# Memory queries and keys as seven-product granules, and attention's token granules as pairs of 512-column products

## The chip, the cores and the metric

One core of a Trainium2 chip. The metric is device time of one launch in microseconds (us), the median of several runs. The engines are named as in the profile: PE is TensorE's matmul stream, PEld its weight loads, DVE is VectorE, ACT is ScalarE, POOL is GpSimd, SP is the engine that issues most DMAs.

## The reference, cut to what matters

The program is one layer of a hybrid trunk over 640 tokens (128 context, 512 latent), width 1024, all in float32: a feed-forward half step, a token mixer, a second feed-forward half step. The mixer multiplies the normed input `h` with one wide input projection and splits the product:

```
mq, mk, mv, mo, mg, dq, dk, dv, gm, gd = split_cols(h @ p['w_in'][l])
att = diff_attention(rope_2d(rmsnorm(dq)), concat(rope_2d(rmsnorm(dk)), cache_k), concat(dv, cache_v), lam)
hm  = rmsnorm(mlstm(mq * 256**-0.5, mk, mv, gates(mg)) forward and backward) * sigmoid(mo)
y   = sigmoid(gm) * (hm @ w_br_m) + sigmoid(gd) * (att @ w_br_d)
x   = x + m[5] * (y @ w_out)
```

`mq`, `mk`, `mv`, `mo` have 4 heads of 256 columns (the memory's queries, keys, values and output gates), `dq`, `dk`, `dv` have 8 attention heads of 128 columns, `gm` and `gd` are branch gates of 1024 columns. So every part is made of pieces of 1024 x 256 weights, which the kernel calls granules. The change is only in how and where the granules of `mq`, `mk`, `mv`, `dq`, `dk` and `dv` are multiplied.

## The kernel before

**Products.** Every float32 operand is split into a high part and a low part of a reduced matmul type (`wH`, `wL`; `hH`, `hL`), and one product is three matmuls, high x high, low x high and high x low (`mm3`; all matmuls of it are recorded at line 75). ACT makes the high part (line 51), DVE the low part (line 54, `wL<-raw,wH`).

**Stages.** The program runs the first feed-forward step; the second norm with the first attention projections; the gates stage; attention; the memory stage (the mLSTM); the two branch products and the output product; and the second feed-forward step.

**Gates stage** (`Gates`, a subclass of the seven-product scheme `Winograd`). A granule is cut into halves along each axis and multiplied by a Strassen-like scheme with seven products in place of eight: 84 matmuls of 320 columns (`ps_f<-`), in place of 96. Its work list holds 12 granules: six of `gm`/`gd`, four of `mo`, and head 0 of `mq` and of `mk`. Results go to DRAM (`gm_dram`, `mq_dram` and so on). Beside it, DVE does "columns" tiles, the adaptive-norm products of a later stage, one behind a granule at the places listed in `IN_GATES`; five more such tiles stand in the memory stage.

**Fill units in attention.** Attention's own work leaves PE waiting for softmax, so the remaining granules stand in a queue (`Fill`) and are multiplied in small units between the pieces of attention. A token granule (`tok_units`) yields [tokens x 256 columns] in five units of 24 matmuls of 256 columns (`ps_t`, 128 tokens each). A feature granule (`feat_units`) yields its transpose in four units of 24 matmuls of 320 columns (`ps_p`). Token granules are `k`, `q` of pairs of heads 1 to 3, `v` of pairs 0 to 3 and `mv` of heads 0 to 3; feature granules are heads 1 to 3 of `mq` and `mk`, and the last of `gm` and of `gd`. The split of the granule at the head of the queue must be complete before its first unit; `ahead()` makes the high part of the next one, `aside()` calls `low()` for its low part, and the slots hold two granules (`wp`, `bufs=2`).

**Attention's order.** For each of 8 heads and 5 query blocks the code writes by hand: scores (`H.scores`: PE, 8 matmuls, `sc`), the turn of the previous block's weights (`ps_wT`), softmax (`H.soft`: DVE's `mn<-sc`, line 1619, then ACT's two `p<-sc,mn` exponentials), fill units, the mix (DVE's `p<-p,r,p`), the values' products (`ps_o`), fill units again. `UNITS` says how many units stand at each place: `two` is one ahead of the mix and one behind the values, `one` is one alone, and the last entry of each head is for the end of the head, where the next head's queries and keys are transposed (`ps_qkT`, 10 small matmuls, then DVE's `kH` casts). When a `k` or `q` granule is finished, `qk_norm_rope` norms and rotates it on DVE (`ss`, `ry`, four multiplies and adds of 128x1024 to 128x1280). Ahead of head 0's first scores stands `gate_rows`, the mLSTM's scans on DVE (scans at line 1409, copy of `QA` and others), one part per call of `aside`. `fill.drain(3)` leaves three granules (12 units) to the memory stage.

**Memory stage.** `load` and `load_c` fetch `P`, `va` and `C` by SP's queue; `cell` is a step of one direction of one head; `fill.pace(0.8, 1)` sets how many units stand between cells; `stats` normalises the output of the last head, and then the branch product `w_brd` follows as fill units.

The scheduler of the language reorders what isn't wrapped in `written()`; PE's and SP's instructions keep the program's order.

## Time and profile before

| what | value |
|---|---|
| median of 3 runs (lowest, highest) | 1813.63 us (1813.38, 1814.05) |
| the profiled execution's own time | 1812.29 us |
| its span in the trace | 1810.5 us, so 1.8 us lie outside the span |
| granted TensorE clock | 1.00 |
| busy share of PE, PEld, DVE, ACT | 99%, 96%, 74%, 50% |

Times in the trace count from the start of the span. A row of the chain of waits is a piece of the work that ended last: start, length, engine and line, how many instructions. A row of a timeline is start, length, instruction, and in brackets how long the engine had been idle and what ended that. A row of the windows has for each stretch of time the busy time of PE, PEld, DVE, ACT and POOL with the number of instructions. Matmul records overlap, so the length of one matmul (309 ns for 320 columns) isn't what it costs: the cost is the distance from start to start, which is read from a row that groups many.

### The profile page before, as it was taken

How to read it: one execution, taken by the hardware profiler on the slowest of the kernel's cores; microseconds unless marked ns; L12 is line 12 of the kernel's file. 1: busy time of each engine (PE TensorE's matmuls, PEld its weight loads, DVE VectorE, ACT ScalarE, POOL GpSimd, SP SyncE). 2: the span in 40 equal slices, each digit the busy share in tenths (PEclk: the TensorE clock that was granted, in tenths of full speed). 3: DMA queues.
4: the chain of work that ended last, by engine and by line, in shares of the span. 5: the costliest groups of instructions: out<-in, count | busy, mean ns of one | idle time of the engine just before them, and what ended most of it. 6: DMA issues, size and time to landing. Idle time of an engine off the chain costs nothing.

```text
span 1810.5 us, 30758 instructions
## 1 busy us (share of the span) xinstructions
PE 1784.8 (99%) x12550; PEld 1743.7 (96%) x12550; DVE 1345.2 (74%) x2162; ACT 899.6 (50%) x1579; POOL 41.0 (2%) x72
## 2 busy tenths in 40 slices
PE   8999999999999999999999999999999999999998
PEld 7999999999999999999999998899999999999998
DVE  6889987677888765858585547877668888897485
ACT  5654544333655455656565546562326545554432
POOL 0000000100000000000000000000000000000010
PEclk9999999999999999999999999999999999999999
DMA  8355566977245544221221134565652455557992
GB/s 327 111 198 177 185 232 224 349 227 266 84 139 182 194 143 131 78 70 63 69 69 60 64 106 129 181 248 209 216 173 78 134 174 185 203 179 274 352 310 84
DMA packets 132207, 311.36 MB, mean 172 GB/s; under 512 B 10017, under 2 KB 93217, under 8 KB 119009
## 3 DMA queue, kind: packets, MB, share of 16 engines
q1 hardware_dynamic: 120690, 263.64, 42.2%
q0 software_dynamic: 10688, 43.13, 7.4%
q8 instruction: 98, 1.61, 0.4%
q10 hardware_dynamic: 688, 2.63, 0.4%
q14 instruction: 43, 0.35, 0.1%
HBM read 240.49 MB, written 68.87 MB: 171 GB/s over the span
## 4 chain that ended last, share of the span: by engine, by line
PE 83%; DVE 7%; DMA 5%; ACT 3%; issue 1%; SPq 0%; DVEq 0%; ACTq 0%
PE ps_f L75 49%; PE ps_p L75 13%; PE ps_t L75 12%; PE sc L75 2%; PE ps_o L75 2%; DVE ww L54 2%; DMA raw_a<-in_w_ada_k 1%; PE ps_qkT L78 1%; PE ps_wT L78 1%; DMA P<-nm_dram 1%; PE ps_n L75 1%; DMA raw<-in_w2b 1%; DVE junk L814 1%; PE ps_u L75 1%; DMA a_raw<-aT_dram 1%
## 5 line engine op out<-in xcount | busy, mean ns | idle before, releaser
L75 PE MATMUL ps_f<-S,ww 128*128 128x320 f32 x2400 | 387.1, 310 | 2.7 <-DMA S<-g_dram 0.9
L75 PEld LDWEIGHTS ps_f<-S,ww 128*128 128x128 f32 x2400 | 359.8, 188 | 6.7 <-DVE ww L54 4.6
L54 DVE TENSOR_TENSOR ww<-raw,ww 128x2048 fp32r<-128x2048 f32 (+1 forms) x73 | 163.9, 2245 | 65.9 <-ACT ww L51 65.8
L75 PE MATMUL ps_t<-wH,hH 128*128 128x256 f32 x640 | 185.1, 289 | 0.9 <-DVE x L57 0.9
L75 PE MATMUL ps_f<-hm,ww 128*128 128x320 f32 x1176 | 185.8, 309 | 0.1
L75 PE MATMUL ps_t<-wH,hL 128*128 128x256 f32 x640 | 181.0, 283 | 0.9 <-DVE hL L54 0.9
L75 PE MATMUL ps_t<-wL,hH 128*128 128x256 f32 x640 | 180.9, 283 | 0.0
L75 PEld LDWEIGHTS ps_f<-hm,ww 128*128 128x128 f32 x1176 | 175.7, 188 | 0.6 <-DVE ww L54 0.6
L51 ACT ACTIVATE ww<-raw 128x2048 fp32r<-128x2048 f32 (+1 forms) x73 | 136.8, 1874 | 58.8 <-DVE raw L54 34.9
L54 DVE TENSOR_TENSOR raw<-raw 128x1024 f32<-128x1024 f32 x186 | 160.8, 864 | 2.4
L75 PE MATMUL ps_f<-hm,wB 128*128 128x320 f32 x1008 | 161.5, 309 | 0.0
L75 PE MATMUL ps_p<-hH,wH 128*128 128x320 f32 x480 | 151.1, 315 | 0.7 <-ACT aT L51 0.7
L75 PEld LDWEIGHTS ps_f<-hm,wB 128*128 128x128 f32 x1008 | 151.3, 188 | 0.0
L75 PE MATMUL ps_p<-hH,wL 128*128 128x320 f32 x480 | 148.3, 309 | 0.0
L75 PE MATMUL ps_p<-hL,wH 128*128 128x320 f32 x480 | 148.3, 309 | 0.0
L51 ACT ACTIVATE u<-ps_f 128x320 f32<-128x320 f32 x129 | 55.8, 433 | 156.1 <-PE ps_f L75 155.9
L75 PEld LDWEIGHTS ps_t<-wH,hH 128*128 128x128 f32 x640 | 122.3, 191 | 1.5 <-ACT nsq L51 1.1
L75 PEld LDWEIGHTS ps_t<-wH,hL 128*128 128x128 f32 x640 | 122.4, 191 | 1.1 <-DVE hL L54 1.1
L75 PEld LDWEIGHTS ps_t<-wL,hH 128*128 128x128 f32 x640 | 122.5, 191 | 0.3
L1619 DVE TENSOR_REDUCE mn<-sc 128x2 f32<-128x1536 f32 (+1 forms) x40 | 59.5, 1488 | 56.0 <-PE sc L75 55.8
L54 DVE TENSOR_TENSOR wL<-raw,wH 128x2048 fp32r<-128x2048 f32 x37 | 84.6, 2288 | 21.6 <-ACT wH L51 21.3
L51 ACT ACTIVATE wH<-raw 128x2048 fp32r<-128x2048 f32 (+1 forms) x45 | 75.4, 1681 | 47.0 <-PE ps_p L75 35.3
(307 smaller groups left out, 3598.9 us busy)
## 6 DMA issues: line engine op xcount, KB each, us to landing
g_dram<-g SPq DMA_DIRECT2D x44, 640.0 KB, 7.5
raw_a<-in_w_ada_c POOLq DMA_DIRECT2D x38, 512.0 KB, 4.8
g_dram<-g SPq DMA_DIRECT2D x24, 480.0 KB, 8.2
raw<-in_w1b SPq DMA_DIRECT2D x11, 1024.0 KB, 4.8
raw<-in_w3b SPq DMA_DIRECT2D x11, 1024.0 KB, 6.4
raw<-in_w1a SPq DMA_DIRECT2D x10, 1024.0 KB, 4.8
raw<-in_w3a SPq DMA_DIRECT2D x10, 1024.0 KB, 6.2
hm<-g_dram SPq DMA_DIRECT2D x7, 1280.0 KB, 11.7
```

What stands on the lines that cost most here:

```text
L51: return placed(nc.scalar.activation(*args, **kw))
L54: return placed(eng.tensor_tensor(out=out, in0=in0, in1=in1, op=op))
L75: tc.keep_in_program_order(nc.tensor.matmul(*args, **kw))
L78: tc.keep_in_program_order(nc.tensor.transpose(*args, **kw))
L814: placed(vec.tensor_tensor_reduce(out=junk, in0=raw, in1=self.csil[:, v, :], op0=ALU.mult, op1=ALU.add, scale=1.0, scalar=0.0, accum_out=m ...
L1619: placed(vec.tensor_reduce(out=mn, in_=sv, axis=AX.X, op=ALU.min))
```

## The change

1. The gates stage has 18 granules: heads 0 to 3 of `mq` and `mk` are all in its work list (six more than before), and all 12 columns tiles stand there; five leave the memory stage. The memory stage loads all `mqT` and `mkT` from DRAM, head 0's and the other keys and queries ahead of the loop over the heads.
2. Ten token granules go in five pairs: `k`+`q` of pairs 1, 2, 3; `v3`+`mv0`; `mv1`+`mv2`. A pair has ten half units of 12 matmuls with 512 columns: unit `(i, h)` multiplies token block `i` with half `h` of the 1024 inputs, for both granules at once; the two half units of a block accumulate in one PSUM bank. `v0`, `v1`, `v2` and `mv3` stay single. Each half of a pair is one raw tile, loaded by two DMAs. Since both halves are needed in turn, a third slot ("x") for splits is added from head 0's third query block on.
3. PSUM: attention's pool of five banks becomes four (`ps2m`) and one for the pairs (`ps2w`, `bufs=1`).
4. `UNITS`: one unit at every query block, and three at the ends of heads 0 to 4, two at the ends of heads 5 and 6. `fill.drain(2)` leaves two granules (8 units) to the memory stage, with `fill.pace(0.6, 1)`.
5. A pair of `k` and `q` is finished by one half unit, so that two `qk_norm_rope` follow each other on DVE.

The core of the diff:

```diff
@@ Fill
+        def pair(self, srcs, units):
+            for half in range(2):
+                self.q.append([(srcs, half), units if half else None, None, None])
+        def load(self, src):
+            if not isinstance(src, tuple):
+                return load_raw(src)
+            raw = rawp.tile([128, 2048], F32, tag="raw", name="raw")
+            srcs, h = src
+            for g in range(2):
+                dma(raw.rearrange("p (k n) -> p k n", n=512)[:, :, 256 * g : 256 * g + 256], srcs[g][:, 4 * h : 4 * h + 4, :])
+            return raw
+        def place(self, i):
+            if self.spare is not None and "x" not in self.live and i + 2 < len(self.q):
+                key, pool = "x", self.spare
+            elif self.live.count("w") < 2:
+                key, pool = "w", wp
+            else:
+                return None
+            self.live.append(key)
+            return [pool.tile([128, 2048], F32R, tag=key + t, name="w" + t) for t in "HL"]
...
@@ one
+            first = self.q[0]
+            wide = first[1] is None
+            g = self.q[1] if wide else first
...
+            if wide and len(g[1]) % 2:
+                self.high(1)
+                while self.low():
+                    pass
...
+            f((first[2], g[2]) if wide else g[2])
+            if wide and len(g[1]) <= 1 or not g[1]:
+                self.live.pop(0)
...
+    def wide_units(psum, evacs):
+        at = [None]
+        def half_unit(ws, i, h):
+            if h == 0:
+                at[0] = wide_ps[0].tile([128, 512], F32, tag="wide", name="ps_t")
+            p = at[0]
+            tok = slice(i * 128, (i + 1) * 128)
+            wh, wl = ws[h]
+            for k in range(4):
+                c, kk = slice(512 * k, 512 * k + 512), 4 * h + k
+                mm3(p, hH[:, kk, tok], hL[:, kk, tok], wh[:, c], wl[:, c], kk == 0, kk == KT - 1)
+            if h:
+                for j, evac in enumerate(evacs):
+                    evac(p[:, 256 * j : 256 * j + 256], i)
+        return [(2.8, lambda ws, i=i, h=h: half_unit(ws, i, h)) for i in range(5) for h in range(2)]
...
+    def wide(*projects):
+        fill.pair([src for src, _ in projects], lambda: wide_units(psum, [make() for _, make in projects]))
     def projections(pr):
-        token(project_k(pr))
-        token(project_q(pr))
+        wide(project_k(pr), project_q(pr))
...
     token(project_v(0))
-    values_of(0)
-    values_of(1)
     projections(1)
-    queries_of_memory(1)
     token(project_v(1))
     projections(2)
-    keys_of_memory(1)
     token(project_v(2))
     projections(3)
-    values_of(2)
-    token(project_v(3))
+    wide(project_v(3), memory_values(0))
+    wide(memory_values(1), memory_values(2))
     values_of(3)
-    queries_of_memory(2)
...
-    keys_of_memory(3, by_act=True)
@@ Gates
-            rest = [(a["w_mq"], mq_dram, 0, self.query), (a["w_mk"], mk_dram, 0, self.plain)]
+            qk = [(a[n], dst, h, f) for h in range(4) for n, dst, f in (("w_mq", mq_dram, self.query), ("w_mk", mk_dram, self.plain))]
...
-    IN_GATES = [(i, 1) for i in range(5, 12)]
+    IN_GATES = [(i, 1) for i in range(5, 17)]
...
+    banks.close()
+    psum = att.enter_context(tc.tile_pool(name="ps2m", bufs=4, space=PSUM, reuse_waits="tile"))
+    wide_ps.append(att.enter_context(tc.tile_pool(name="ps2w", bufs=1, space=PSUM, reuse_waits="tile")))
...
-    two, one = (1, 1), (1, 0)
-    UNITS = {
-        0: (two, two, two, two, one, (1, 1, 1)), 1: (two, two, two, one, one, (0,)),
...
+    one = (1, 0)
+    UNITS = {hd: (one,) * 5 + ((1, 1, 1),) for hd in range(7)}
+    UNITS[5] = UNITS[6] = (one,) * 5 + ((1, 1, 0),)
+    UNITS[7] = (one,) * 4 + ((0, 0), (0, 0))
...
-            fill.drain(3)
+            fill.drain(2)
...
+    load_keys(0)
+    load_queries(0)
...
-    fill.pace(0.8, 1)
+    fill.pace(0.6, 1)
...
-    columns.place(5, csil2, load_columns_raw, 1)
+    for h in range(1, 4):
+        load_keys(h)
+        load_queries(h)
```

DVE's order at the opening of attention, before the change: `kH` are the casts of head 0's transposed keys, `QA`, `keep` and `lf` belong to `gate_rows`, and `wL` is the low part of the third granule in the queue (`mv1`), whose first unit stands behind head 0's first scores.

```order
720 L1595 CAST kH<-ps_qkT 128x2x256
721 L1414 COPY bl<-b 32x5
722 L1595 CAST kH<-ps_qkT 128x2x256
723 L1595 CAST kH<-ps_qkT 128x2x128
724 L1434 COPY QA<-u 64x640
725 L1399 COPY keep<-b 32x3
726 L1400 COPY keep<-b 32x3
727 L54 TENSOR_TENSOR wL<-raw,wH 128x2048
728 L1409 SCALAR_TENSOR_TENSOR lf<-keep,u 4x128 x2
```

The same place in the changed kernel:

```order
782 L1460 MEMSET lf 64x640
783 L1473 COPY bl<-b 32x5
784 L1651 CAST kH<-ps_qkT 128x2x256 x2
785 L1651 CAST kH<-ps_qkT 128x2x128
786 L1493 COPY QA<-u 64x640
787 L1458 COPY keep<-b 32x3
788 L1459 COPY keep<-b 32x3
789 L1468 SCALAR_TENSOR_TENSOR lf<-keep,u 4x128
790 L54 TENSOR_TENSOR wL<-raw,wH 128x2048
791 L1468 SCALAR_TENSOR_TENSOR lf<-keep,u 4x128
```

The low part has moved behind one scan, and it is now the second half of pair 1, whose half units `(0, 1)` and `(1, 1)` stand on PE ahead of head 0's first scores.

DVE's order in head 1 before the change, where `k` of pair 1 has been finished and is rotated (`k_tok`, `rope`); each `mn` is the softmax's maximum of one query block, here of the second and third:

```order
788 L1619 TENSOR_REDUCE mn<-sc 128x2
789 L57 SCALAR_TENSOR_TENSOR ry<-rt,ry 128x20
790 L54 TENSOR_TENSOR k_tok<-k_tok,ry 128x1280
791 L54 TENSOR_TENSOR k_tok<-k_tok,g_kn 128x256
792 L1633 RECIPROCAL rc<-sm 128x2
793 L57 SCALAR_TENSOR_TENSOR r<-sm,nlam,rc 128x1
794 L57 SCALAR_TENSOR_TENSOR p_7804<-p_7805,r,p_7804 128x768
795 L54 TENSOR_TENSOR rope<-rope,ropeBk 128x1024
796 L54 TENSOR_TENSOR k_tok<-k_tok,ropeAk 128x1024
797 L61 TENSOR_SCALAR ao<-ps_o,rc 128x128
798 L54 TENSOR_TENSOR k_tok<-k_tok,rope 128x1024
799 L1619 TENSOR_REDUCE mn<-sc 128x2
```

And in the changed kernel, from the first large multiply of `k`'s rotation; the two `mn` are those of the first and second query block, and the `ss` at the end is the first step of `q`'s rotation:

```order
847 L54 TENSOR_TENSOR k_tok<-k_tok,ry 128x1280
848 L1675 TENSOR_REDUCE mn<-sc 128x2
849 L54 TENSOR_TENSOR ao<-ao,ry 128x640
850 L54 TENSOR_TENSOR k_tok<-k_tok,g_kn 128x256
851 L54 TENSOR_TENSOR rope<-rope,ropeBk 128x1024
852 L54 TENSOR_TENSOR k_tok<-k_tok,ropeAk 128x1024
853 L1689 RECIPROCAL rc<-sm 128x2
854 L54 TENSOR_TENSOR k_tok<-k_tok,rope 128x1024
855 L57 SCALAR_TENSOR_TENSOR r<-sm,nlam,rc 128x1
856 L57 SCALAR_TENSOR_TENSOR p_8236<-p_8237,r,p_8236 128x768
857 L1675 TENSOR_REDUCE mn<-sc 128x2
858 L1536 TENSOR_REDUCE ss<-rope 128x20
```

What moved: the first large multiply of `k` stands ahead of the first block's maximum, where it stood behind the second's, and `q`'s rotation begins behind the second block's maximum; before, it began behind the third's and a split.

More of the change, by code (lines that the diff above doesn't have):

```diff
@@ L1260, in high @@
                 g = self.q[i]
-                raw = load_raw(g[0]) if g[3] is None else g[3]
-                g[2] = h, lo = [wp.tile([128, 2048], F32R, tag="w" + t, name="w" + t) for t in "HL"]
+                t = self.place(i)
+                if t is None:
+                    return
+                raw = self.load(g[0]) if g[3] is None else g[3]
+                g[2] = h, lo = t
                 act(h, raw, AF.Copy)
@@ L1277, in ahead @@
         def ahead(self):
-            for i in range(2):
+            for i in range(4):
                 if self.high(i):
                     break
-            if len(self.q) > 2 and self.q[2][3] is None:
-                self.q[2][3] = load_raw(self.q[2][0])
+            if sum(g[2] is None and g[3] is not None for g in self.q) < 2:
+                for g in self.q[:6]:
+                    if g[2] is None and g[3] is None:
+                        g[3] = self.load(g[0])
+                        break
         def one(self):
@@ L1465, in rope_place @@
     def rope_place(of):
-        if not in_pools:
+        if not late_p:
             return rope_p[0].tile([128, 5, 256], F32, tag="pk", name="rope", bufs=2)
-        return pair(of, 2, "rope").rearrange("p a b -> p (a b)").rearrange("p (t n) -> p t n", t=5)
+        return late_p[0].tile([128, 5, 256], F32, tag="rope", name="rope")
     at_rope = [None]
@@ L2006, in tile_trunk @@
             H.finish_norm()
-            if odd:
-                for i in range(5):
-                    fill.one()
-                    if i in (0, 1):
-                        N.keys(i)
-                    if i == 1:
-                        with written():
-                            fill.ahead()
-            else:
-                N.keys(0)
-                fill.units(n[1])
-                N.keys(1)
-                with written():
-                    fill.ahead()
-                fill.units(n[2])
+            N.keys(0)
+            fill.units(n[1])
+            N.keys(1)
+            with written():
+                fill.ahead()
+            fill.units(n[2])
             late = H.finish
```

62 lines of the change are left out of this document (22 added, 40 removed).

## The prediction

> **What bounds the kernel now.** I read the page's first part, then the windows cut at the stages' borders, then the chain of waits row by row, and for the places that the change touches DVE's timeline.
>
> ```profile
> span 1810.5 us, 30758 instructions
> PE 1784.8 (99%) x12550; PEld 1743.7 (96%) x12550; DVE 1345.2 (74%) x2162; ACT 899.6 (50%) x1579; POOL 41.0 (2%) x72
> ...
> 504.00:652.30 148.30, 148.30 (x1013) 148.30 (x1013) 116.52 (x154) 76.48 (x115) 3.71 (x7) 1.00 0.52 180
> 652.30:1074.60 422.30, 416.55 (x3339) 406.25 (x3338) 276.51 (x429) 232.38 (x486) 0.00 (x0) 1.00 0.23 76
> 1074.60:1207.00 132.40, 127.68 (x727) 113.65 (x727) 101.54 (x327) 79.56 (x216) 0.00 (x0) 1.00 0.54 171
> ```
>
> PE is the bound in all three stages. The gates stage (first window) leaves it no gap; attention (second) has 422.30 - 416.55 = 5.75 us without a matmul, the memory stage (third) 4.72. So each product taken away is worth its full time as long as PE still has work when a softmax or a split is late; the fill units are that work, and the change takes many of them out of attention. The prices come from the chain of waits:
>
> ```profile
> 504.28 148.15 PE ps_f L75 x1010
> ...
> 652.42 8.64 PE ps_t L75 x72
> ...
> 668.50 5.81 PE ps_t L75 x48
> ...
> 680.94 1.39 PE sc L75 x8
> 682.34 5.75 PE ps_t L75 x48
> ...
> 690.14 2.87 PE ps_t L75 x24
> 693.01 1.34 PE ps_o L75 x12
> ...
> 733.82 2.87 PE ps_t L75 x24
> 737.23 2.87 PE ps_t L75 x24
> ...
> 751.85 3.52 PE ps_p L75 x24
> ...
> 791.76 1.41 PE sc L75 x8
> 793.19 1.77 DVE mn L1619
> 794.99 1.89 ACT p L51 x4
> 796.91 1.67 PE sc L75 x8
> ...
> 948.48 1.40 PE sc L75 x8
> ```
>
> A product of 320 columns costs 148.15 / 1010 = 0.1467 us, and a feature unit 24 of them, 3.52. A token unit of 24 products of 256 columns takes 2.87, 0.1196 each. Eight score products, four of 512 and four of 256 columns, take 1.39: (1.39 - 4 x 0.1196) / 4 = 0.228 for one of 512, or 0.235 from rows of 1.40 and 1.41 and a last product that drains. I take 0.232, so a half unit is 12 x 0.232 = 2.79.
>
> **The change part by part.** *Products.* The gates stage gains six granules of 84 products: 504 x 0.1467 = +73.9. Attention loses five feature granules (heads 1 to 3 of the queries, 1 and 2 of the keys), 20 x 3.52 = -70.4; the memory stage loses the sixth, 4 x 3.52 = -14.1. Fifty token units become fifty half units: 50 x (2.79 - 2.87) = -4.0; with 0.228 it would be -6.7, with 0.235 -2.5. Floor: 73.9 - 70.4 - 14.1 - 4.0 = -14.6.
>
> The row bears on a rule of the Trainium skill ("TensorE: Matmul & The Clock Gate", "Wait — 56ns, not 53.3ns?"): a warm product takes its columns over 2.4 GHz and some 2.5 ns. By it 24 products of 256 columns would cost 2.62 and 12 of 512 2.59 us, so that the pairs would be worth an estimated 1.6 us in all and not 4.0. The trace's products are 7 to 10% slower than the skill's at each of the three widths, at a granted clock of 1.00, and the rows decide.
>
> *Gates stage.* In before DVE is busy 116.52 of 148.30 us beside 12 granules and 7 tiles. With 18 granules and 12 tiles the ratio stays (0.58 tiles a granule, now 0.67), so some 10 of a granule's 12.35 us: PE stays the bound, 0 (up to +4).
>
> *Opening of attention.* In before the second granule's two units stood ahead of the first scores; now it is two blocks of pair 1, whose second half needs its own low part, the `wL` below:
>
> ```profile
> 661.91 1.56 DVE L54 TENSOR_TENSOR kp<-k_tok,kpk 128x640 fp32r<-128x640 f32 x2 [2.00 <-PE ps_qkT L78]
> ...
> 673.52 2.29 DVE L54 TENSOR_TENSOR wL<-raw,wH 128x2048 fp32r<-128x2048 f32 x1
> 675.73 0.83 DVE L1409 TENSOR_TENSOR_SCAN lf<-keep,u 4x128 f32<-4x128 f32 x2
> 676.59 2.58 DVE L1409 TENSOR_TENSOR_SCAN lf<-keep,m,u 4x512 f32<-4x512 f32 x2
> ...
> 683.11 1.74 DVE L1619 TENSOR_REDUCE mn<-sc 128x2 f32<-128x1536 f32 x1
> ```
>
> From 661.91 to 683.11 DVE has no idle time, and the order shows the same work ahead of `wL` and one scan more (0.83 / 2 = 0.42). So that low part is there at 673.52 + 2.29 + 0.42 = 676.2. PE would want it when the first half unit is done, 668.50 + 2.79 = 671.3. Stall 4.9; 4.0 to 5.5, since nothing on PE can pass it. I take +4.9.
>
> *First query block of each head.* The rows from 791.76 to 796.91 are the chain of scores, maximum, exponentials, next scores: 5.15 us in which nothing else ends last, and it recurs whatever PE does, because the scores have one place. Between the two groups of scores PE has the scores (1.40), one unit and the transposes of the block before (737.23 - 733.82 - 2.87 = 0.54): with half units 1.40 + 2.79 + 0.54 = 4.73, a stall of 0.42; in head 0, which has no such transposes, 0.96. Before, heads 0, 1, 3, 5, 6, 7 had two units there. The rows end at the last handover and leave out 0.1 to 0.3 of semaphores; six heads make 0.96 + 5 x 0.42 = 3.1 to 5. I take +4.0. At the later blocks one unit and the values' products (1.34) stand beside the chain, 1.40 + 0.54 + 2.79 + 1.34 = 6.1 against 5.15: PE stays the bound, with 1 us in hand.
>
> *Two rotations in a row.* That 1 us is what DVE has in hand too, and here is one rotation in head 5:
>
> ```profile
> 938.27 2.28 DVE L54 TENSOR_TENSOR wL<-raw,wH 128x2048 fp32r<-128x2048 f32 x1
> 940.47 1.48 DVE L1477 TENSOR_REDUCE ss<-rope 128x20 f32<-128x1280 f32 x1
> ...
> 942.32 1.02 DVE L57 SCALAR_TENSOR_TENSOR p<-p,r,p 128x768 f32<-128x768 f32 x1
> 943.26 0.34 DVE L61 TENSOR_SCALAR ao<-ps_o,rc 128x128 f32<-128x128 f32 x1
> ...
> 945.69 1.49 DVE L54 TENSOR_TENSOR q_tok<-q_tok,ry 128x1280 f32<-128x1280 f32 x1
> ...
> 949.15 1.22 DVE L54 TENSOR_TENSOR rope<-rope,ropeBq 128x1024 f32<-128x1024 f32 x1
> 950.28 1.22 DVE L54 TENSOR_TENSOR q_tok<-q_tok,ropeAq 128x1024 f32<-128x1024 f32 x1
> 951.41 1.75 DVE L1619 TENSOR_REDUCE mn<-sc 128x2 f32<-128x1536 f32 x1
> 953.08 1.22 DVE L54 TENSOR_TENSOR q_tok<-q_tok,rope 128x1024 f32<-128x1024 f32 x1
> ```
>
> Large steps: 1.48 + 1.49 + 3 x 1.22 = 6.6, with the small ones some 7.5. The scores were done at 948.48 + 1.40 = 949.88 and their maximum began at 951.41, 1.5 late. Attention's 5.75 us of gaps are for the most part this (heads 1, 3 and 5), some 4.7. Now `k` and `q` are done at once, 15 us of rotation that the order puts into the first three blocks, 18 us in which a maximum, a mix (1.02), an output (0.34) and lesser steps already need 3 x 3.5. That is 25 against 18 and the end of the head before; three heads lose up to 7 each, but the end of the head, with some 9 us of units and transposes, takes the first 4 of it. I take 3.4 a head, 10.2 in all, +5.5 over before; 0 if the end of the head hides it, +12 if not.
>
> *Ends of heads.* Heads 5 and 6 have no unit behind the last transposes, so their evacuation stands bare ahead of the scores: between 0 and the 2.87 of the unit that covered it. Nearest to casts and lower parts of about a microsecond, +1.1 each, +2.2.
>
> *The pairs' one bank.* The next block's first half unit waits for two evacuations:
>
> ```profile
> L51 ACT ACTIVATE v_tok<-ps_t x20: 361/384/388, 658.3 to 982.6; 128x256 f32<-128x256 f32 x20
> ```
>
> Two of 0.38 and a handover, 0.96. Within a head, scores, transposes and values (3.3 us) stand between and hide it; at the ends of heads only transposes do, and 5 to 8 such places leave 0.1 to 0.2 each: +1.0 (0 to 3).
>
> The Trainium skill has a rule against one bank ("PSUM — Partial Sum Buffer", "Summary: rules for kernel authors"): reading PSUM while a matmul runs wants a different bank. Where that cover fails the sum would be 25 x 0.96 = 24 us worse by it; no row before shows a bank of one in attention's loop, so the cover is argued from the code's order.
>
> *Memory stage.* Beside the 14.1 above, five tiles leave DVE. The wait for `P` at its start goes or stays; at its end, the chain that norms the last head shows:
>
> ```profile
> 1079.90 11.68 DMA P<-nm_dram
> ...
> 1207.31 10.55 PE ps_p L75 x72
> ...
> 1208.10 0.48 DVE L57 SCALAR_TENSOR_TENSOR hs<-ps_n,den,hs 128x256 f32<-128x256 f32 x1
> ...
> 1213.31 2.07 DVE L57 SCALAR_TENSOR_TENSOR hs<-hs,ry,g_mh 128x256 f32<-128x256 f32 x5
> ```
>
> Until the first of the five `hs` is done, 1213.31 + 2.07 / 5 = 1213.7, PE had three units from 1207 on. Left are 8 units for 40 cells' slots, and by PE's order one unit (3.52) stands there: 1213.7 - 1207.0 - 3.5 = +3.2. The later loads stand behind more loads on SP, and fewer units are there to hide a late `P` at 1079.90 + 11.68; the DVE work that leaves gives some of it back, -0.7. I take +2.5 (-1 to +8).
>
> *Sum.* -14.6 + 4.9 + 4.0 + 5.5 + 2.2 + 1.0 + 2.5 = +5.5. On the profiled execution's 1812.29 that is 1817.8; its time is 1.3 below the median of 1813.63, so against the median **1819.1 us**, 0.3% slower. A measurement of this kernel tells about 0.2% from no change, 3.6 us.
>
> **The rivals.**
>
> *A, the floor wins.* Of the stalls only the opening's is certain; the rest are places where I let DVE be late while over 422 us it is busy 276.51. If the scheduler's order lets rotations fall into head ends, and the first blocks lose their 3.1, the sum is -14.6 + 4.9 + 3.1 + 1 = -5.6: 1808.0; with the opening alone 1803.9. For it: few gaps before, although heads 2 and 4 already ran with one unit a block. Against it: just those heads show the chain as the last to end at 791.76.
>
> *B, break-even.* Rotations cost nothing extra and the memory stage's end is covered: 5.5 - 5.5 - 2.5 = -2.5, 1811.1; with half of each +1.5, 1815.1.
>
> *C, DVE falls behind for good.* If in heads 1, 3 and 5 each rotation is paid in full, 3 x 7 - 4.7 = +16 and not +5.5, the sum is +16, 1829.6. It decides where DVE's share over a head's first three blocks passes 95%. For it: the maximum 1.5 late with one rotation. Against it: the slack at ends of heads.
>
> *D, pairs that save nothing.* A 512-column product costs two of 256, 0.239: the sum is +9.5, 1823.1. Against it: the score rows, 0.228 to 0.235.
>
> **How the numbers follow.** Stalls as I sum them, +20.1, lie between some 9 and 32 by the bounds above. My forecast (stalls of 17 to 25, 1816 to 1824) has 0.42, A 0.22, B 0.24, C 0.09, D 0.03. The range leaves out A's lower third and C's upper half: 1805 to 1829. Faster by over 0.2% (below 1810.0) needs stalls under 11, which is A: 0.22. Within 0.2% (to 1817.3) are B and the low edge of the forecast: 0.29. Slower: 0.49.
>
> **What would show it.** Right: the gates stage 74 us longer with no gap; 512-column products 0.232 us apart; PE without a matmul for about 5 us ahead of the second half unit of pair 1 with `wL` as releaser; gaps of 0.4 to 1 us before the second scores of heads; attention 57 us shorter (422 to 365) with 18 us more of gaps; the memory stage 11 to 12 us shorter. Wrong: attention below 357, an opening without a stall, or DVE ahead of the scores in heads 1, 3 and 5.

## The result, and the profile after

The changed kernel takes 1835.18 us, median of 4 runs (1833.63 to 1835.58), against 1813.51 (1812.36 to 1814.05, 4 runs): a ratio of 1.0119 (1.0101 to 1.0136), 21.7 us or 1.2% slower. The forecast was 1819.1, within 1805 to 1829. The profiled execution took 1835.11 with a span of 1833.3, 22.8 longer than before; the sum had 5.5.

The page's first part after the change:

```profile
span 1833.3 us, 29601 instructions
...
PE 1784.0 (97%) x11878; PEld 1710.1 (93%) x11878; DVE 1374.5 (75%) x2196; ACT 915.5 (50%) x1605; POOL 43.5 (2%) x77
```

PE is as busy as before (1784.8) with 672 records fewer, and idle for some 24 us more. The windows at the stages' borders (gates, attention, memory stage, branch products); the last three columns are the granted clock, the busy share of the DMA engines and GB/s:

```profile
506.60:728.60 222.00, 222.00 (x1515) 222.00 (x1515) 171.71 (x221) 109.97 (x163) 6.33 (x12) 1.00 0.53 177
728.60:1105.30 376.70, 352.23 (x2260) 308.88 (x2259) 262.35 (x417) 216.75 (x467) 0.00 (x0) 0.98 0.23 76
1105.30:1237.20 131.90, 123.34 (x705) 110.86 (x703) 94.66 (x315) 84.60 (x231) 0.00 (x0) 0.99 0.57 191
1237.20:1386.00 148.80, 148.09 (x995) 147.84 (x996) 96.92 (x167) 46.62 (x62) 6.33 (x12) 0.98 0.55 196
```

The gates stage is 74 us longer with no gap, as forecast. Attention is 376.7 and not 365: it has 376.70 - 352.23 = 24.5 us of gaps (before 5.75; 18 more were forecast), so the gaps are of the size foreseen, and yet it is 11 us too long. About half of that (5.4 us, added up below) shows in the column of the granted clock: 0.98, 0.99 and 0.98 where before stood 1.00. The chain of waits shows where the unforeseen waits are:

```profile
506.73 211.36 PE ps_f L75 x1441
...
732.12 3.05 DMA gm_dram<-g_out
735.63 2.01 DMA m<-in_state_m
...
755.26 2.19 DVE wL L54
757.50 4.38 PE ps_t L75 x11
...
775.94 2.77 PE ps_t L75 x12
...
1225.03 6.21 DMA raw<-in_w_brd
...
1237.92 5.66 PE ps_p L75 x24
1243.80 3.52 PE ps_p L75 x24
```

A product of the gates stage still costs 211.36 / 1441 = 0.1467, and a half unit 2.77 where 2.79 was forecast. But a store of the gates stage and a load of one column (`m`) stand on the chain ahead of attention, a weight load ahead of the branch products, and two rows are too long: eleven products in 4.38 us (0.40 each), and a unit of 24 in 5.66, the next one in 3.52.

**The opening of attention.** `gate_rows` loads the gates' bias `b_g` and the old state `m0`. SP's timeline before (start, length, instruction), and after:

```profile
653.30 1.07 SPq L97 DMA_DIRECT2D b_g<-in_b_gate  x1
...
655.06 0.99 SPq L1831 DMA_DIRECT2D gm_dram<-g_out  x2
```

```profile
731.47 1.03 SPq L1873 DMA_DIRECT2D gm_dram<-g_out  x2
735.25 0.33 SPq L97 DMA_DIRECT2D b_g<-in_b_gate  x1
```

Before, `b_g` was issued ahead of the last two stores of `g_out`, 1 us after the stage's end. Now it comes, with `m0` behind it, 3 us behind the issue of those stores, just when the last has landed (732.12 + 3.05 = 735.17): the pool of the gate rows lies where `g_out` was. ACT and PE after it (in brackets the idle time ahead of the instruction, and what ended it):

```profile
737.64 0.52 ACT L51 ACTIVATE fg<-ps_g,b_g 64x320 f32<-64x320 f32 x1 [4.42 <-DMA m<-in_state_m]
```

```profile
741.00 0.75 PE L78 MATMUL ps_qkT<-identr,qpk 128*128 128x128 f32 x4 [3.29 <-ACT v_tok L51]
742.65 0.50 PE L78 MATMUL ps_qkT<-identr,qpk 128*128 128x128 f32 x2 [0.91 <-ACT v_tok L51]
...
757.50 0.53 PE L75 MATMUL ps_t<-wL,hH 128*128 128x512 f32 x1 [2.64 <-DVE wL L54]
...
927.31 0.87 PE L78 MATMUL ps_wT<-ident,p 128*128 128x128 f32 x6 [2.26 <-DVE p L57]
...
1237.23 0.69 PE L78 MATMUL ps_hT<-ident,hs 128*128 128x128 f32 x2 [5.62 <-DVE hs L57]
```

ACT works in order: `fg` waits for the load, and behind it, from 740.56 on, stand the evacuations of `v_tok` that free the banks PE needs. PE loses 3.29 + 0.91 = 4.2 us before the forecast wait, for `wL`, comes at all. The windows behind the gaps:

```profile
743.00:750.80 7.80, 7.80 (x50) 7.80 (x49) 7.29 (x11) 1.48 (x4) 0.00 (x0) 0.71 0.01 2
...
928.51:931.92 3.41, 3.41 (x10) 2.63 (x9) 0.81 (x4) 1.06 (x6) 0.00 (x0) 0.50 0.00 0
...
1237.50:1243.40 5.90, 5.90 (x26) 5.90 (x26) 1.75 (x5) 3.68 (x3) 0.00 (x0) 0.57 1.03 425
```

PE has no gap in any of them and yet works slowly. The two token units of the first take 7.87 us where two cost 5.75; the eleven products at 757.50 take 4.38, 0.16 of it the last one's drain, so 4.22 - 11 x 0.232 = 1.7 too much; the products in the second window lose some 1.6; the unit in the third takes 5.84 against 3.59 in a kernel without the gap (e6 below). Four gaps are followed by 2.1 + 1.7 + 1.6 + 2.3 = 7.7 us of loss at a granted clock near one half, the first three of them in attention (5.4); before had no such place.

**The memory stage's end.** ACT there:

```profile
1231.26 1.91 ACT L51 ACTIVATE wH<-raw 128x2048 fp32r<-128x2048 f32 x1 [1.31 <-DMA raw<-in_w_brd]
1233.08 0.40 ACT L51 ACTIVATE hjunk<-hs 128x256 f32<-128x256 f32 x1
...
1235.61 0.21 ACT L51 ACTIVATE rt<-rv 128x5 f32<-128x5 f32 x1 [1.50 <-DVE rv L63]
```

The split of a weight granule of the branch products stands ahead of the last two of the five sums of squares (`hjunk`) that the last head's norm needs. It waits for its load, and the sums wait behind it, though their data have long been there. Then DVE makes the low part of the same granule (1233.20 to 1235.49) ahead of `rv`, for which `rt` waits 1.50 us.

### The profile page after: what moved, and what is told of

Read it like the earlier page. It is cut to its first block, busy times and chain, and to the rows that moved or that the text cites. A ratio compares the mean times of both kernels' runs of the same rounds, so it can differ in the third digit from the quotient of the medians.

```text
span 1833.3 us, 29601 instructions
## 1 busy us (share of the span) xinstructions
PE 1784.0 (97%) x11878; PEld 1710.1 (93%) x11878; DVE 1374.5 (75%) x2196; ACT 915.5 (50%) x1605; POOL 43.5 (2%) x77
## 4 chain that ended last, share of the span: by engine, by line
PE 79%; DVE 10%; DMA 5%; ACT 5%; issue 1%; SPq 0%; DVEq 0%; ACTq 0%
PE ps_f L75 50%; PE ps_p L75 10%; PE ps_t L75 8%; PE sc L75 2%; DVE ww L54 2%; PE ps_n L75 2%; PE ps_o L75 2%; DMA raw<-in_w2b 2%; DMA raw_a<-in_w_ada_k 1%; DVE mn L1675 1%; ACT p L51 1%; PE ps_u L75 1%; PE ps_wT L78 1%; PE ps_qkT L78 1%; DVE junk L814 1%
## 5 line engine op out<-in xcount | busy, mean ns | idle before, releaser
L54 DVE TENSOR_TENSOR raw<-raw 128x512 f32<-128x512 f32 (+1 forms) x204 | 176.8, 867 | 2.8
L75 PE MATMUL ps_t<-wH,hH 128*128 128x256 f32 (+1 forms) x440 | 153.6, 349 | 2.5 <-ACT wT L51 1.6
L75 PE MATMUL ps_t<-wL,hH 128*128 128x256 f32 (+1 forms) x440 | 148.2, 337 | 2.6 <-DVE wL L54 2.6
L75 PE MATMUL ps_t<-wH,hL 128*128 128x256 f32 (+1 forms) x440 | 148.8, 338 | 0.9 <-DVE hL L54 0.9
L814 DVE CUSTOM_DVE_ANT_0 junk<-raw_a,csil 128x1024 bf16<-128x1024 f32 (+1 forms) x86 | 104.8, 1219 | 4.5 <-DMA raw_a<-in_w_ada_c 4.3
L54 DVE TENSOR_TENSOR wB<-raw,wB 128x1024 fp32r<-128x1024 f32 x70 | 85.5, 1221 | 26.3 <-ACT wB L51 26.3
L75 PEld LDWEIGHTS ps_t<-wH,hH 128*128 128x128 f32 x440 | 85.2, 194 | 11.1 <-ACT wT L51 2.0
L51 ACT ACTIVATE wB<-raw 128x1024 fp32r<-128x1024 f32 x70 | 73.6, 1051 | 41.8 <-DMA raw<-in_w2a 15.7
L75 PE MATMUL ps_p<-hH,wH 128*128 128x320 f32 x288 | 90.0, 313 | 0.7 <-DVE y L54 0.7
L75 PE MATMUL ps_p<-hH,wL 128*128 128x320 f32 x288 | 89.0, 309 | 0.0
L75 PE MATMUL ps_p<-hL,wH 128*128 128x320 f32 x288 | 89.0, 309 | 0.0
## 6 DMA issues: line engine op xcount, KB each, us to landing
hm<-g_dram SPq DMA_DIRECT2D x7, 1280.0 KB, 12.7
```

The costliest lines, as they stand in the source:

```text
L51: return placed(nc.scalar.activation(*args, **kw))
L54: return placed(eng.tensor_tensor(out=out, in0=in0, in1=in1, op=op))
L75: tc.keep_in_program_order(nc.tensor.matmul(*args, **kw))
L814: placed(vec.tensor_tensor_reduce(out=junk, in0=raw, in1=self.csil[:, v, :], op0=ALU.mult, op1=ALU.add, scale=1.0, scalar=0.0, accum_out=m ...
```

## The experiments

Three theories were on record ahead of the first runs: 1, the loss is at three places (the rows' late inputs and the second half's split, both at the opening, and a split ahead of the statistics at the memory stage's end), to which the expectations for e2 and e3 add the rotations; 2, the pairs slow attention as a whole; 3, moving the six granules costs it, and the pairs are worth their 4 us and nothing more. Stage lengths in us are those of each kernel's profiled execution; "over" is the median over that of the kernel before in the same comparison (1813.27, 1812.06 or 1812.15). The profiled executions of e8 and e9 (1824.39 and 1824.65) were the shortest of their four, 3 to 4 us under the medians.

| kernel | median | over | ratio (interval) | opening | attention | memory | branch |
|---|---|---|---|---|---|---|---|
| before | 1813.51 | 0 | 1 | 28.5 | 422.4 | 143.0 | 145.3 |
| after | 1835.18 | 21.7 | 1.0119 (1.0101-1.0136) | 39.6 | 376.7 | 131.9 | 148.7 |
| e1_rows_early | 1829.29 | 16.0 | 1.0092 (1.0074-1.0110) | 35.7 | 371.5 | 130.8 | 148.8 |
| e2_pair1_single | 1839.58 | 26.3 | 1.0146 (1.0131-1.0161) | 34.1 | 377.3 | 136.7 | 148.0 |
| e3_no_pairs | 1835.70 | 22.4 | 1.0127 (1.0110-1.0144) | 33.3 | 376.2 | 136.6 | 146.8 |
| e4_split_late | 1831.88 | 18.6 | 1.0108 (1.0093-1.0123) | 39.0 | 375.1 | 130.9 | 148.7 |
| e6_stats_first | 1824.73 | 12.7 | 1.0071 (1.0055-1.0086) | 39.1 | 376.7 | 127.0 | 145.4 |
| e7_warm_end | 1830.08 | 18.0 | 1.0101 (1.0084-1.0117) | 38.1 | 375.2 | 130.5 | 146.7 |
| e8_rows_after_split | 1828.49 | 16.4 | 1.0088 (1.0071-1.0105) | 29.6 | 367.0 | 130.7 | 148.8 |
| e9_no_q_rotation | 1828.07 | 16.0 | 1.0090 (1.0071-1.0109) | 37.4 | 368.5 | 130.7 | 148.7 |
| e10_all | 1817.69 | 5.5 | 1.0033 (1.0020-1.0046) | 29.6 | 368.8 | 127.6 | 145.5 |
| e11_all_single | 1824.62 | 12.5 | 1.0072 (1.0058-1.0085) | 28.5 | 371.4 | 128.8 | 146.4 |
| e12_all_pool | 1821.33 | 9.2 | 1.0053 (1.0041-1.0066) | 29.6 | 372.9 | 126.9 | 145.5 |

**The rows' loads early (e1).**

```diff
+    early_rows = [load(gq_p, [128, 1], a["b_gate"], name="b_g"), load(gq_p, [64, 1], a["state_m"], name="m0")]
...
-        b_g = load(gt, [128, 1], a["b_gate"], name="b_g")
-        m0 = load(gt, [64, 1], a["state_m"], name="m0")
+        b_g, m0 = early_rows
...
-    gt = gates.enter_context(tc.tile_pool(name="gates", bufs=1))
+    gt = gates.enter_context(tc.tile_pool(name="gates", bufs=1, reuse_waits="tile"))
```

> Edit: the two small inputs of gate_rows (b_g and m0) are loaded ahead of the gates stage into a pool that lives through attention, and the pool of the rows releases space tile by tile. Theory 1 (three places: the rows' late inputs with the slow clock behind them, the second half's split at the opening, a split ahead of the statistics at the memory stage's end): the 4.3 us without a matmul ahead of head 0's first keys and the 2.1 us that the next two units lose to a lower clock go, 5 to 6.5 us faster than the changed kernel, about 1829. Theory 2 (the pairs slow all of attention): no such gap matters, within 1.5 us of the changed kernel, 1834 to 1837, since the time comes back at the next wait for a split. If only the load was late and the rows' space is what is waited for, half of it stays: 1832.

The median came 5.7 us nearer to before, as theory 1 expected. The first gap is gone, so PE reaches the second half unit of pair 1 earlier and waits longer for `wL`. PE in e1:

```profile
752.59 0.79 PE L75 MATMUL ps_t<-wL,hH 128*128 128x512 f32 x1 [4.58 <-DVE wL L54]
```

This is the wait that the prediction put at 4.9, alone: 4.58. But the products behind it run at half clock again (0.50 from 751.34 to 758.16), ten of them 0.43 apart, 2 us more. The opening became 3.9 us shorter.

**Pair 1 as two single granules (e2), and all pairs undone (e3).**

```diff
-    projections(1)
+    token(project_k(1))
+    token(project_q(1))
```

```diff
-        fill.pair([src for src, _ in projects], lambda: wide_units(psum, [make() for _, make in projects]))
+        for project in projects:
+            token(project)
...
-    psum = att.enter_context(tc.tile_pool(name="ps2m", bufs=4, space=PSUM, reuse_waits="tile"))
-    wide_ps.append(att.enter_context(tc.tile_pool(name="ps2w", bufs=1, space=PSUM, reuse_waits="tile")))
+    psum = att.enter_context(tc.tile_pool(name="ps2m", bufs=5, space=PSUM, reuse_waits="tile"))
```

> Edit: k and q of pair 1 are two single granules, the other four pairs stay. Theory 1: the 4.4 us wait for the second half's low part at the opening goes, the rotations of head 1 come apart (1 to 3 us), five half units' saving is lost (+0.8): 4.5 to 6.5 us faster than the changed kernel, 1829 to 1831. Theory 2 (pairs slow each head): a fifth of the pairs' cost goes with one of five pairs, some 3 to 4 us, without the opening getting shorter. If the next thing that is late at the opening takes the wait's place (the rows on DVE): under 1.5 us, 1834 to 1835.

> Edit: all five pairs undone, token granules single again, five banks in the common pool; order of the granules, units at each place and the 18 granules of the gates stage as in the changed kernel. Theory 1: the opening's wait for the split goes (-4.4), the rotations come apart (-3 to -5 in heads 1, 3, 5), the pairs' saving is lost (+4): 1829 to 1832, the memory stage's end as late as in the changed kernel. Theory 2: nearly all of the 21.7 us go, 1813 to 1818. Theory 3 (moving the six granules costs it, pairs are worth their 4 us and nothing more): 1838 to 1840.

e2 went the other way. Its opening is 5.5 us shorter, but head 0 takes 48.6 and not 41.4 us: a single `k` is finished earlier, and its rotation now falls into head 0's blocks of one unit. DVE and PE there:

```profile
785.59 1.22 DVE L54 TENSOR_TENSOR rope<-rope,ropeBk 128x1024 f32<-128x1024 f32 x1
...
789.91 1.02 DVE L57 SCALAR_TENSOR_TENSOR p<-p,r,p 128x768 f32<-128x768 f32 x1
```

```profile
791.08 1.51 PE L78 MATMUL ps_wT<-ident,p 128*128 128x128 f32 x6 [4.06 <-DVE p L57]
...
792.60 0.41 PE L75 MATMUL ps_t<-wL,hH 128*128 128x256 f32 x1
```

The mix (`p`) stands behind the three large steps of the rotation, PE waits 4.06 us, and the products behind it run at half clock (0.41 against 0.28). In e2 and e3 the first load of `P` also lands some 5 us later behind the other keys, which is the memory stage's 136.7. e3 has the same two costs without any pair and is no faster than after (22.4 over against 21.7). None of the three expectations for e3 came true; theory 2 had it win most of the loss back. With both costs in it, e3 does not yet say what pairs are worth; e11 below does.

**The split behind the sums of squares (e4), and behind the whole statistics (e6).** In e4 the split of the second branch granule comes behind the fifth `hjunk`; in e6 behind the last step of the reciprocal root on ACT, and the low part behind the first `hs`.

```diff
+            fill.eager = i > 0
+            if i == 1:
+                with tc.issue_after(mem[3].at_stats.ins):
+                    fill.prefetch(1)
```

```diff
+            fill.eager = i > 0
+            if i == 1:
+                with tc.issue_after(mem[3].at_stats.ins), tc.issue_after(mem[3].at_hs.ins):
+                    fill.prefetch(1)
+                    fill.low()
```

> Edit: at the end of the memory stage the split of the second branch granule is placed behind the last statistics on ACT. Theory 1: the statistics no longer stand behind a split that waits for its load; the 5.9 us gap ahead of the last head's first transposes shrinks to 2 to 3 and the next unit, 5.8 us in the changed kernel, runs at its 3.6: 5 to 6 us faster, 1829 to 1830. Rival: the second granule's split is now late in its turn and its unit waits instead: within 1.5 us of the changed kernel.

> Edit: as e4, but the second branch granule's split stands behind the whole of the last head's statistics, the two small ACT steps of the reciprocal root and the first scaled block included; in e4 it still stood ahead of those two steps. Theory 1: the gap ahead of the last head's first transposes, 5.9 us in the changed kernel and 5.1 in e4, falls to 1.5 to 2.5 us, too short to lower the clock, so that the next unit takes 3.6 and not 5.8: 5.5 to 6.5 us faster than the changed kernel, about 1829.5. Rival: the statistics' own chain is what is late, and the gap stays at 4 us or more: within 2 us of the changed kernel.

e4 missed: PE's gap is 4.83 instead of 5.62, where 2 to 3 were expected, and the unit behind it still slow. ACT in e4, and in e6:

```profile
1227.57 1.91 ACT L51 ACTIVATE wH<-raw 128x2048 fp32r<-128x2048 f32 x1
1229.39 0.19 ACT L51 ACTIVATE rt<-rv 128x5 f32<-128x5 f32 x1
```

```profile
1228.56 0.21 ACT L51 ACTIVATE rt<-rv 128x5 f32<-128x5 f32 x1 [0.24 <-DVE rv L63]
...
1228.92 1.90 ACT L51 ACTIVATE wH<-raw 128x2048 fp32r<-128x2048 f32 x1
```

In e4 the split only changed places with the sums and still stood ahead of the two small steps `rt` and `ry`, and its low part ahead of DVE's steps behind `ry`. In e6 both stand behind them, and PE and the window behind its gap are:

```profile
1230.18 0.44 PE L78 MATMUL ps_hT<-ident,hs 128*128 128x128 f32 x2 [1.28 <-DVE hs L57]
```

```profile
1230.20:1234.00 3.80, 3.80 (x27) 3.79 (x28) 3.72 (x5) 1.90 (x2) 0.00 (x0) 1.00 0.99 408
```

The gap fell from 5.62 to 1.28, the clock stayed at 1.00 and the unit took 3.59; memory stage and branch products together are 8.2 us shorter, the median 9.0 nearer to before. That is more than the 5.5 to 6.5 expected: gap and unit account for 4.3 + 2.3 = 6.6, the rest is not placed. The expectation called gaps of up to 2.5 us too short to lower the clock, which after's own 2.26 contradicts; the gap that came was 1.28. The cause at this place is shown.

**Products without use in the gap (e7).** In after's gap stand 44 matmuls of 128 columns on a spare bank, so that PE is idle for less of it, while the statistics stay as late as they were.

```diff
             fill.one()
+            if i == 0:
+                warm = psum.tile([128, 512], F32, tag="mm", name="ps_warm")
+                for _ in range(44):
+                    mm(warm[:, :128], identr, identr, start=True, stop=True)
```

> Edit: 44 matmuls of 128 columns whose result nobody reads, some 2.5 us of PE, stand in the gap ahead of the last head's first transposes; the gap's cause is left alone. If the unit behind the gap is slow because PE was idle (clock theory): the transposes start when they did, the next unit takes 3.6 and not 5.8 us, 2.2 us faster than the changed kernel, about 1833. Rival: the unit is slow for a cause of its own (operands late, DMA traffic): no change, 1834.5 to 1836.

```profile
1227.94 5.02 PE L75 MATMUL ps_warm<-identr 128*128 128x128 f32 x44
```

```profile
1230.26:1233.67 3.41, 2.71 (x25) 2.56 (x23) 2.79 (x6) 1.83 (x7) 0.00 (x0) 1.00 1.00 409
...
1234.20:1239.20 5.00, 5.00 (x26) 5.00 (x27) 1.91 (x5) 3.83 (x4) 0.00 (x0) 0.71 1.03 422
```

About half of the expected gain came: the next unit took 4.77 instead of 5.84, at a granted clock of 0.71. Narrow products in the gap shortened the slow stretch, from 6.83 to 3.41 us, and did not prevent it: PE was busy for 2.71 of the 3.41 us up to 1233.67, and from there the clock stood at 0.50 until 1237.09. The 44 took 5.02 us where 2.5 were expected, 0.114 each, hardly less than a product of 256 columns (0.120). Whether a PE that is busy with so few columns is idle for the clock stays open. The median came 3.7 nearer to before, more than the 2.2 expected; 1.5 us of it lie in attention, which this edit does not touch.

**The rows behind the split (e8).** e1's edit, and every part of the gate rows from the third on comes on DVE behind pair 1's low part.

```diff
     fill.units(2)
+    at_split = fill.at_low
...
             for _ in range(ROWS.get((qi, part), 0)):
-                next(rows, None)
+                with ExitStack() as st:
+                    if qi > 0:
+                        st.enter_context(tc.issue_after(at_split.ins))
+                    next(rows, None)
```

> Edit: e1's, and gate_rows' steps from the third part on stand behind the opening's second split on DVE. In e1 the wait for that split was 4.9 us and a lower clock behind it cost 2 more. Theory 1 (the order on DVE is what delays the split): gap of 1 to 2 us, no lower clock: 4 to 6 us faster than e1 at the opening, of which head 0's blocks give back 1 to 3 as the rows now stand between its maxima: 1825 to 1828. Rival (DVE's total work is what bounds opening and head 0 together): what the opening gains head 0 loses, 1828 to 1830 as in e1.

The low part is now done at 748.86, and e1's was at 752.54. PE in e8:

```profile
748.92 0.50 PE L75 MATMUL ps_t<-wL,hH 128*128 128x512 f32 x1 [1.14 <-DVE wL L54]
...
919.24 0.85 PE L78 MATMUL ps_wT<-ident,p 128*128 128x128 f32 x6 [2.97 <-DVE p L57]
```

The opening is 29.6, 1.1 above before, with head 0 at 41.7 against 41.4: the moved rows cost nothing there. So nearly the whole loss of the opening was order, not work; e10 below has the same 29.6. The median alone would not have shown it: it is 16.4 over, where e1's was 16.0, inside the rival's range, and no trace says where the other three executions lost their 4 to 5 us. Head 3 of e8 holds a gap of 2.97 us, and so does that of e10, with different ends: behind it e8 ran at 1.00 and e10 at 0.50. Their windows, cut into pieces of 3.41 us (the last section says why), e8's first:

```profile
914.09:917.50 3.41, 2.18 (x17) 1.85 (x16) 3.41 (x6) 2.61 (x8) 0.00 (x0) 1.00 0.00 0
917.50:920.91 3.41, 1.67 (x11) 1.53 (x12) 2.92 (x6) 2.96 (x6) 0.00 (x0) 1.00 0.00 0
```

```profile
915.05:918.46 3.41, 0.46 (x4) 0.27 (x4) 3.41 (x7) 2.60 (x5) 0.00 (x0) 1.00 0.00 0
918.46:921.87 3.41, 3.40 (x11) 2.98 (x12) 1.79 (x6) 1.80 (x7) 0.00 (x0) 0.50 0.00 0
```

In e10 nearly the whole gap lies in one piece; in e8 a border at 917.50 cuts it into 1.23 and 1.74.

**Without the second rotation (e9).** The kernel leaves out the norm and rotation of `q` for pairs 1 to 3.

```diff
-                if i == 4:
+                if i == 4 and pr == 0:
                     now(lambda: qk_norm_rope(t, tabs[0]))
```

> Edit: the changed kernel without the norm and rotation of q for the head pairs 1 to 3 (left out: their queries go in raw); k's rotation stays. It prices the second rotation of each pair. My forecast's price for both was 10.2 us in heads 1, 3, 5, of which 4.7 were there before. Theory A (rotations in one-unit blocks bind DVE): heads 1 and 3 fall from 46.6 and 45.5 us to 43 to 44, 4 to 7 us faster, 1828 to 1831. Theory B (the ends of heads hide the second rotation): within 2 us of the changed kernel.

Head 3 in after, on DVE: the large steps of `q`'s rotation (here the first) stand between the maximum (`mn`) and the mix (`p`), which ends at 927.25; PE's row at 927.31 above is its waiter.

```profile
919.74 1.75 DVE L1675 TENSOR_REDUCE mn<-sc 128x2 f32<-128x1536 f32 x1
...
921.73 1.22 DVE L54 TENSOR_TENSOR rope<-rope,ropeBq 128x1024 f32<-128x1024 f32 x1
...
926.24 1.01 DVE L57 SCALAR_TENSOR_TENSOR p<-p,r,p 128x768 f32<-128x768 f32 x1
```

Head 3, with the same 268 products, in after and in e9:

```profile
899.47:944.93 45.46, 42.21 (x268) 36.96 (x267) 33.33 (x52) 25.54 (x56) 0.00 (x0) 0.96 0.14 46
```

```profile
894.98:936.06 41.08, 40.66 (x268) 35.91 (x267) 26.67 (x42) 23.03 (x52) 0.00 (x0) 1.00 0.16 50
```

Heads 1, 3 and 5 go from 46.6, 45.5 and 39.0 to 45.7, 41.1 and 38.2: 6.1 us in all, 1.6 of it the slow stretch in head 3. So the second rotations do cost time, and most of it in one head.

**e8 and e6 together (e10), the same without pairs (e11), with a part of the rotations on POOL (e12).** e10 has both edits as shown. e11 adds e3's edit and lets `P` go ahead of the other keys' loads, so that neither of e3's costs is in the way; e12 adds to e10:

```diff
-        tt(vec, s4, s4, B[:, :, None, :].to_broadcast([128, 4, 4, 64]), ALU.mult)
+        tt(nc.gpsimd if late_p else vec, s4, s4, B[:, :, None, :].to_broadcast([128, 4, 4, 64]), ALU.mult)
```

> Edit: the changed kernel with e8's two edits (the rows' inputs early, the rows behind the split) and e6's (the second branch granule's split behind the statistics). By stages e8 took 9.7 us out of attention and e6 8.2 us out of the memory stage's end and the branch products. Theory 1 (two ends of stages, each with its own cause, independent): 1835.2 - 17.9 = 1817, within 0.3% of the kernel before and still not faster, since the rotations and first blocks that the forecast named remain. Rival (the ends were only where a common lag shows): the sum doesn't add up, 1822 or more.

> Edit: e10 with all five pairs undone (single token granules, five common banks) and the memory's later keys and queries loaded behind P, as in e3 three key loads stood ahead of it. With the other stalls out, this prices the pairs alone. By e3's heads, 304.6 us from the first scores of head 0 to those of head 7 against 298.7 with pairs, and 4.0 us of products among it: theory (pairs worth their products, and the order of the rotations decides the rest): 3 to 7 us slower than e10, 1820 to 1824. Rival (the pairs are what made the change slower): faster than e10, 1808 to 1815.

> Edit: e10, and one of the three large multiplies of each rotation of pairs 1 to 3 runs on POOL. If DVE's load in the blocks with rotations is what stalls heads 1, 3 and 5 (theory A): 1.2 us less of DVE in each of six rotations, 2 to 5 us faster than e10, 1812 to 1815. If POOL's step is slow and the later steps wait for it, or POOL's work slows DVE's: as e10 or slower, 1817 to 1825.

e10 is close to where it was expected: 16 of the 21.7 us are won back at the two ends, where the stages' lengths of e8 and e6 promised 18, by order alone. Theory 3 falls for that part, and theory 1 holds for its three places, which all lie at the two ends. It is still 5.5 us slower than before (1.0020 to 1.0046). e11 is 7 us slower than e10: freed of what hid it, the pairs are worth having, mostly because a single `k` puts its rotation into head 0 (48.4 against 41.9). That rules theory 2 out. e12 lost 3.6 to e10; the moved multiply there:

```profile
L54 POOL TENSOR_TENSOR rope<-rope,ropeBk 128x1024 f32<-128x1024 f32 x3 | 8.2, 2740 | 240.8 <-ACT rope L51 240.8
```

2.74 us on POOL against DVE's 1.22, on a path that waits for it: head 1 went from e10's 46.6 to 50.0. No kernel was faster than before.

## Why the prediction was wrong, step by step

**Right.** The floor: gates +73.9 against 73.9, half units 2.77 against 2.79, attention's gaps 18.7 us more against 18 (opening 6.8 against 4.9, heads 11.8 against 12.7). The opening's wait for `wL`: 4.58 in e1, where nothing else covers it, against 4.9. The memory stage is 11.1 shorter, against 11.6, but that is luck: its last wait is 2.4 longer than the step had it, the rest of the stage 1.9 shorter. The first blocks' chain shows where it was put: PE's row at 773.56 waits 1.03 us for ACT's `p`, against 0.96. Rival D (pairs that save nothing) is out by the half units' 2.77 against 2.87; no wait for the pairs' one bank stands among PE's gaps over half a us. C's price came near to the result, but its mechanism did not: heads 1, 3 and 5 don't pay 16 us.

Two slips of the working weigh little: 12 x 0.232 is 2.78, and the estimate of 1.6 us for the pairs is 50 x 0.03 = 1.5.

**Wrong.** The span is 17.3 us above the sum. By stages:

- *The opening, +6.5.* The step "Opening of attention" counted one wait, for the split. It looked at DVE's order and not at SP's: the loads of `b_g` and `m0` now wait for stores, and through ACT's order PE waits 4.2 us. The slow products behind the two gaps cost 2.1 + 1.7. The foreseen wait was 2.64 instead of 4.9, since the first gap hid part of it. 4.2 + 3.8 - 2.3 = 5.7; 0.8 is not placed.
- *The heads, +4.6.* 1.6 are the slow stretch in head 3. The other 3.0 are not in PE's gaps. From head 0's first scores to the stage's end the windows before and after are

```profile
680.78:1074.66 393.88, 388.07 (x3095) 377.77 (x3093) 253.80 (x393) 218.15 (x461) 0.00 (x0) 1.00 0.22 72
```

```profile
768.24:1105.32 337.08, 319.45 (x2061) 279.35 (x2060) 237.04 (x373) 200.67 (x439) 0.00 (x0) 0.99 0.22 71
```

  so the gaps grew from 5.8 to 17.6, by 11.8 where the four terms of the heads had 12.7. In heads 1, 3 and 5 they are 3.4 before (the step "Two rotations in a row" read some 4.7) and 8.3 after (it had 10.2). So the 3.0 are time in which PE counts as busy; each wait also costs the drain of the product ahead of it (0.16 above), and there are more waits, but no run separates this.
- *The end of the memory stage with the products behind it, +3.9.* The step had 3.2 for the statistics' own chain. It missed that ACT has a split ahead of two of the sums, and DVE its low part ahead of `rv`: the wait is 5.6 (+2.4), and the slow unit behind it costs 2.3; -0.8 is spread over both stages.
- *The start of the program, +2.5,* which the change doesn't touch; this start varies from 504.1 to 506.8 between the profiles. In after the clock stood at one half from 34.21 to 37.63, before it did not; of such a stretch at most half, 1.7 us, is loss.

One omission runs through all of them: **every wait was priced at its own length.** The granted clock of 1.00 in before was taken as given; before has no gap over 1.4 us in these stages. Of the 17.3 us some 7.7 are products at half clock behind four gaps, and up to 1.7 the same thing at the start. Some 4.3 (4.2 - 2.3 + 2.4) come from queues that work in order, SP's, ACT's and at the end DVE's, in which something not needed yet stands ahead of something urgent. The heads' 3.0 stay open.

**What remains.** e10 measures the forecast's +5.5, but by chance: against the forecast its opening is 3.5 us better and its memory stage with the branch products 3.6, its heads 6.7 worse (1.7 of that the slow stretch in head 3); where the heads' time goes stays open. By the sum, the change saves 14.6 us of products; attention has, even in e10, some 16 us more of gaps than before (21.55 against 5.75). What moved was the cover.

## What to carry to other kernels

Fill work has a second value beside its own time: it keeps the matmul clock up. When a change takes it away, list every new PE gap over about 2 us, and shorter ones that stand close together, and add some 2 us to each that may be followed by a slow stretch (here 1.6 to 2.3). Then read the order of all queues at a stage's border, small loads and weight splits included, and ask of each urgent instruction what stands ahead of it and what that waits for.

## What was not expected of the hardware

The granted clock falls after gaps of little over 2 us, and not each time. It fell after 2.08 (e1), 2.26, 2.64, 3.29 + 0.91, 4.58 and 5.62 us; the same gap of 2.97 in head 3 was followed by half clock in e10 and not in e8, and neither was after's own gap of 2.03 in head 1.

What decides is when the gap lies. In after's trace the clock stands at 0.50 from 740.77 to 747.60, 757.84 to 761.25, 928.51 to 931.92 and 1235.71 to 1242.53 us. Each of these stretches is 3.41 or 6.83 us long, and their starts lie 17.07, 170.67 and 307.20 us apart, which is 5, 50 and 90 times 3.413. So in this trace the clock changes only at the borders of pieces of 3.41 us that run on whatever PE does; in the other traces the borders are counted from their own stretches (e8's starts at 1224.70, e9's at 740.34). The piece ahead of the third stretch, which holds the gap of 2.26:

```profile
925.10:928.51 3.41, 1.20 (x9) 1.12 (x10) 3.25 (x7) 2.89 (x6) 0.00 (x0) 1.00 0.00 0
```

PE had gone on at 927.31, 1.2 us before the clock fell. The pieces of the gaps named here that were followed by half clock had PE busy for 0.00 to 1.33 us, the highest in e1; those that were not had 1.66 (after, 2.03) and 1.67 (e8), and 1.48 in e9, where a border cuts a gap of 3.45 in two. This is no sharp line: in attention e2 and e3 have three pieces with 1.74 to 1.80 us of busy PE, and e7 has the one with 2.71, that half clock followed.

The Trainium skill ("TensorE: Matmul & The Clock Gate", "What's actually happening") says that the clock is halved after at least one idle window of about 3.4 us and restored after about as long a busy one, and that the window runs freely. The borders, the lengths of the stretches and the two ends of the same gap agree with that. That the whole window has to be idle does not: the clock was halved after windows with 1.20 and 1.33 us of work in them, and the measurement decides.

The spread between runs of one kernel goes in part with this. e1's four runs took 1825.98, 1828.56, 1830.03 and 1833.59 us at mean granted clocks of 0.997, 0.994, 0.994 and 0.993, and 0.004 of 1830 us are 7.3 of the 7.6 between the ends. But e8's shortest and longest, 1824.39 and 1829.31, both had 0.996.

The Trainium skill ("TensorE: Matmul & The Clock Gate", "Architectural detail: the array is 16× 32×32, not 1× 128×128") says that the queues of ACT and DVE are strictly in order. The traces agree: in after two sums of squares, ready to run, stood behind a split that waited 1.31 us for its load.
